# Attention scores: narrow products joined, the forget bias moved to the key side, and a different split of buffers

## The chip, the cores and the metric

The kernel runs on one core of one Trainium2 chip. Its time is device microseconds of one launch; three runs are given by their median. A profile of one more execution of the same program is the source of every row below. The engines are TensorE (PE; its weight loads are PEld), VectorE (DVE), ScalarE (ACT), GpSimd (POOL) and SyncE (SP, which here only issues DMAs).

## The reference

Two layers of a hybrid decoder block over 256 tokens, 1024 features. Each layer: a half-step SwiGLU FFN, a mixing block, a second half-step FFN, a gated per-layer input; a final RMSNorm. The mixing block runs an RG-LRU branch beside a forgetting attention of 8 heads of 128:

```python
log_f = jax.nn.log_sigmoid((f_logit + f_b).astype(jnp.float32))
dcum = jnp.cumsum(log_f, axis=1).transpose(0, 2, 1)
s = jnp.einsum('bhqd,bhkd->bhqk', qb, kh).astype(jnp.float32) * scale
s = s + dqb[..., None] - dcum[:, :, None, :]
s = jnp.where(kpos[None, :] <= qpos[:, None], s, -jnp.inf)
pr = jax.nn.softmax(s, axis=-1).astype(vh.dtype)
return jnp.einsum('bhqk,bhkd->bhqd', pr, vh)
```

The bias of a score is the difference of two cumulative sums, one of the query's position and one of the key's. A softmax over the keys does not change when a number that depends on the query alone is added to its row.

## The kernel before

**Precision.** Every f32 operand is split into a high part (rounded to the matmul's input type) and the low rest: ACT writes the high part, DVE subtracts it to get the low one. A product is then three matmuls, high by high, high by low, low by high. Where high and low of the moving operand lie side by side in one 512-column tile, two matmuls do (`mm2`, lines 344 to 347: one of 512 columns, one of 256), else three of 256 (`mm3`, lines 304 to 306).

**Weights.** `Weights` streams all weight matrices through SBUF in the order of a plan of 238 chunks, 1024 KB each, or 704 KB for the FFNs' output matrices. SP loads a chunk into a raw buffer (tag `wr`, line 84, three buffers); ACT and DVE split it in two units (lines 95 and 96) into one of five pairs of unit buffers (`wh`, `wl`); PE reads the pairs, 4 units behind the splits. A raw buffer is free for the next load when DVE has ended its second split; a unit buffer when PE has read it. Two more matrices per layer (`apart`, line 101, tile `wra`) pass through the same raw buffers in the middle of the FFNs' output stages and are split into tiles of their own (`wbh`, `wbl`). The first layer's input and first weights (tiles `hd`, lines 184 and 186) use the raw buffers too.

**Attention.** For each head four steps stand between other products (the `filler` products of the gates, tiles `f`, and the last query and key projections, tiles `qk`): `step_a` transposes q and k (tile `tr`) and splits them (tiles `aq`), and makes on ACT (line 702) the weights of the bias product from the cumulative sums; `step_b` makes the scores: for the first 128 queries four matmuls against 128 keys, for the second 128 queries four against 256 keys, each time three of `mm3` and one with the bias (line 711). Only keys that a block can see are computed, so the first block has half the columns. DVE then masks and takes the row minimum in one operation (line 715), ACT takes the exponential and its sum (line 717), DVE multiplies by the reciprocal of the sum (line 721, twice). `step_c` transposes the probabilities (tile `pt`, line 729), `step_d` multiplies by v.

**Order.** The order of each engine's instructions is not the order of the code: a scheduler plays the program through with its own model of times and buffers and writes each engine's queue. Each queue then runs strictly in that order, and an instruction that waits holds up all that stand behind it on its engine.

Of the kernel before, what the change touches and what calls it, by code (L numbers as in the profile page):

```python
# [10 lines left out]
F32 = mybir.dt.float32  # L11
F32R = mybir.dt.float32r
AF = mybir.ActivationFunctionType
ALU = mybir.AluOpType
AX = mybir.AxisListType

P = 128
# [102 lines left out]
def trunk(ctx: ExitStack, tc: tile.TileContext, head, xT, pT, vec, w1i, w1o, wf, wqk, wv, wg, wro, wao, wo, w2i, w2o,  # L120
# [12 lines left out]
    def nm(s):  # L133
        cnt[0] += 1
        return f"{s}{cnt[0]}"
# [2 lines left out]
        return bp.tile(shape, dt, name=nm(s), tag="big")  # L138

    def work(dt=F32, s="w"):  # L140
        return kp.tile([P, 256], dt, name=nm(s), tag="w", bufs=12)

    def work2(dt=F32, s="w2"):
        return kp.tile([P, 512], dt, name=nm(s), tag="w2", bufs=3)

    def small(n, s="s", tag="small"):
        return kp.tile([P, n], F32, name=nm(s), tag=tag, bufs=16)
# [12 lines left out]
    for l in range(DEPTH):  # L160
# [8 lines left out]
        plan += [(w2i[l, j], [1024, 1024]) for j in range(FT)]  # L169
        plan += [(w2o[l, m, :, h * 1408:(h + 1) * 1408], [768, 640]) for m in range(KT) for h in range(2)]  # L170
        plan += [(wpg[l, c], [1024, 1024]) for c in range(4)]
    W = Weights(nc, wp, plan, ahead=4, raw_bufs=3, unit_bufs=5, big=big)


    x = cp.tile([P, KT, S], F32, name="x")
# [1 line left out]

    hd = []
    for i in range(KT // 2):
        t = wp.tile([P, 2, HC], F32, name=f"hd{i}", tag="wr", bufs=W.raw_bufs)  # L180
        hd += [t[:, 0], t[:, 1]]
        if i == 0:
            for k in range(2):
                nc.sync.dma_start(out=t[:, k], in_=head[:, k])
        else:
            nc.sync.dma_start(out=t, in_=head[:, 2 * i:2 * i + 2])
# [13 lines left out]

    tri = cp.tile([P, S], F32R, name="tri")

    acol = cp.tile([P, NH], F32, name="acol")
    mcol = cp.tile([P, NH], F32, name="mcol")
    grp = cp.tile([P, 4], F32, name="grp")
    sel = cp.tile([P, 3], F32, name="sel")
    lfh = cp.tile([P, TT, P], F32R, name="lfh")
    lfl = cp.tile([P, TT, P], F32R, name="lfl")
    NRX = 3
# [24 lines left out]
    def constants():  # L234
        G.memset(mask, 0.0)
        G.affine_select(out=mask[:, P:], in_=mask[:, P:], pattern=[[-1, P]], compare_op=ALU.is_ge, fill=BIG,
                        base=0, channel_multiplier=1)
        trif = work(s="trif")
        G.memset(trif, 1.0)
        G.affine_select(out=trif[:, :P], in_=trif[:, :P], pattern=[[1, P]], compare_op=ALU.is_ge, fill=0.0,  # L240
                        base=0, channel_multiplier=-1)
        G.memset(lfh.bitcast(F32), 0.0)
        G.memset(lfl.bitcast(F32), 0.0)
        for t in rxp:
            G.memset(t[:, 0:3], 0.0)
        V.tensor_copy(out=tri, in_=trif)
        yield
        V.tensor_tensor(out=acol, in0=ident[:, 0:NH], in1=ident[:, 32:32 + NH], op=ALU.add)
        V.tensor_tensor(out=mcol, in0=ident[:, 64:64 + NH], in1=ident[:, 96:96 + NH], op=ALU.add)
        V.tensor_scalar(out=mcol, in0=mcol, scalar1=-1.0, scalar2=None, op0=ALU.mult)  # L250
        yield
        for g in range(4):
            V.tensor_reduce(out=grp[:, g:g + 1], in_=ident[:, 32 * g:32 * g + 32], axis=AX.X, op=ALU.add)
        yield
        V.tensor_tensor(out=sel[:, 0:1], in0=grp[:, 1:2], in1=grp[:, 3:4], op=ALU.add)
        V.tensor_scalar(out=sel[:, 0:1], in0=sel[:, 0:1], scalar1=-1.0, scalar2=None, op0=ALU.mult)
        V.tensor_tensor(out=sel[:, 1:2], in0=grp[:, 0:1], in1=grp[:, 1:2], op=ALU.add)
        V.tensor_tensor(out=sel[:, 2:3], in0=grp[:, 2:3], in1=grp[:, 3:4], op=ALU.add)
        yield
        V.tensor_scalar(out=half, in0=vt[:, :, HALF0:], scalar1=0.5, scalar2=None, op0=ALU.mult)  # L260
        for l in range(DEPTH):
            V.tensor_tensor(out=gqk[:, l:l + 1], in0=vt[:, l, VEC["gq"]:VEC["gq"] + 1],
                            in1=vt[:, l, VEC["gk"]:VEC["gk"] + 1], op=ALU.mult)
            ls = small(KT)
            yield from log_sigmoid(ls, vt[:, l, VEC["lam"]:VEC["lam"] + KT], KT)
            yield
            V.tensor_scalar(out=sp[:, l, 0], in0=ls, scalar1=-4.0, scalar2=None, op0=ALU.mult)
            V.tensor_scalar(out=sp[:, l, 1], in0=ls, scalar1=4.0, scalar2=None, op0=ALU.mult)
# [234 lines left out]
    def mix(l, n, wgp):  # L503
# [101 lines left out]
            tick(2)  # L605


        dc = kp.tile([P, S], F32R, name=nm("dc"), tag="dc", bufs=1)
        dk = kp.tile([P, S], F32R, name=nm("dk"), tag="dk", bufs=1)

        def forget():
            lf = kp.tile([P, TT * NH], F32, name=nm("lf"), tag="lf", bufs=1)
            yield from log_sigmoid(lf, z, TT * NH)
            yield
            lf3 = lf.rearrange("p (t o h) -> p t o h", t=TT, o=1)
            for t in range(TT):
                oh = lfh[:, t].rearrange("p (g c) -> p g c", g=4)[:, :, 0:NH]
                ol = lfl[:, t].rearrange("p (g c) -> p g c", g=4)[:, :, 0:NH]
                V.tensor_copy(out=oh, in_=lf3[:, t].to_broadcast([P, 4, NH]))
                V.tensor_tensor(out=ol, in0=lf3[:, t].to_broadcast([P, 4, NH]), in1=oh.bitcast(F32), op=ALU.subtract)  # L620
            yield
            yield
            dps = atbank("dc")
            T.matmul(dps[:, 0:S], lhsT=lfh[:, 0], rhs=tri, start=True, stop=False, skip_group_check=True)
            T.matmul(dps[:, 0:S], lhsT=lfl[:, 0], rhs=tri, start=False, stop=False, skip_group_check=True)
            T.matmul(dps[:, P:S], lhsT=lfh[:, 1], rhs=tri[:, 0:P], start=False, stop=False, skip_group_check=True)
            T.matmul(dps[:, P:S], lhsT=lfl[:, 1], rhs=tri[:, 0:P], start=False, stop=True, skip_group_check=True)
            dh = work(F32R, "dh")
            A.activation(out=dh, in_=dps[:, 0:S], func=AF.Copy)
            V.scalar_tensor_tensor(out=dc, in0=dh.bitcast(F32), scalar=sel[:, 0:1], in1=dps[:, 0:S], op0=ALU.mult,  # L630
                                   op1=ALU.add)
            V.tensor_scalar(out=dk, in0=dc.bitcast(F32), scalar1=sel[:, 1:2], scalar2=sel[:, 2:3], op0=ALU.mult,
                            op1=ALU.add)


        qk = [None, None]
# [50 lines left out]
        def step_a(h):  # L687
            s = st[h]
            cb, hh = h // 4, h % 4
            ps = atbank("tr")  # L690
            for w in range(2):
                for t in range(TT):
                    T.transpose(ps[:, (w * TT + t) * P:(w * TT + t + 1) * P], qk[cb][:, w, t, hh * P:(hh + 1) * P], ident)
            s["q"] = qh, ql = awork(S, "aq", 5), awork(S, "aq", 5)
            s["k"] = kh, kl = awork(S, "aq", 5), awork(S, "aq", 5)
            s["b"] = awork(S, "aq", 5)
            g = gqk[:, l:l + 1]
            A.activation(out=qh, in_=ps[:, 0:S], func=AF.Copy)
            A.activation(out=kh, in_=ps[:, S:], func=AF.Copy, scale=g)
            V.tensor_tensor(out=ql, in0=ps[:, 0:S], in1=qh.bitcast(F32), op=ALU.subtract)  # L700
            V.scalar_tensor_tensor(out=kl, in0=ps[:, S:], scalar=g, in1=kh.bitcast(F32), op0=ALU.mult, op1=ALU.subtract)
            A.activation(out=s["b"], in_=dc.bitcast(F32), func=AF.Identity, scale=mcol[:, h:h + 1], bias=acol[:, h:h + 1])

        def step_b(h):
            s = st[h]
            (qh, ql), (kh, kl), bl = s["q"], s["k"], s["b"]
            ps = atbank("s")
            for t, o, nk in ((0, 0, P), (1, P, S)):
                q = slice(t * P, (t + 1) * P)
                mm3(ps[:, o:o + nk], qh[:, q], ql[:, q], kh[:, 0:nk], kl[:, 0:nk], True, False)  # L710
                T.matmul(ps[:, o:o + nk], lhsT=bl[:, q], rhs=dk[:, 0:nk], start=False, stop=True)
            sv = pr = awork(384, "pr", 2, F32)
            mx, rs = small(TT, "mx", "sa"), small(TT, "rs", "sa")
            for t, o, nk in ((0, 0, P), (1, P, S)):
                V.tensor_tensor_reduce(out=sv[:, o:o + nk], in0=ps[:, o:o + nk], in1=mask[:, S - nk:S], scale=1.0,
                                       scalar=3e38, op0=ALU.add, op1=ALU.min, accum_out=mx[:, t:t + 1])
                A.activation(out=pr[:, o:o + nk], in_=sv[:, o:o + nk], func=AF.Exp, scale=-1.0, bias=mx[:, t:t + 1],
                             accum_out=rs[:, t:t + 1])
            V.reciprocal(out=rs, in_=rs)
            for t, o, nk in ((0, 0, P), (1, P, S)):  # L720
                V.tensor_scalar(out=pr[:, o:o + nk], in0=pr[:, o:o + nk], scalar1=rs[:, t:t + 1], scalar2=None,
                                op0=ALU.mult)
            s["p"] = pr

        def step_c(h):
# [309 lines left out]
```

## Time and profile before

| | |
|---|---|
| median of three runs | 1322.99 us (1322.96 to 1323.09) |
| the profiled execution | 1323.63 us |
| its span, first to last instruction | 1321.8 us |
| PE busy, DVE busy, ACT busy | 99%, 81%, 62% |
| mean granted TensorE clock | 0.997 |
| DMA | 240.21 MB, mean 182 GB/s |

The profiled execution is 0.64 us over the median, and 1.8 us of it lie around the span. A busy share of PE is a weak sign by itself, since matmuls overlap in the pipeline and the end of each is modelled; the distance from one start to the next is what a matmul costs the stream.

### The profile page before, as it was taken

How to read it: one execution, taken by the hardware profiler on the slowest of the kernel's cores; microseconds unless marked ns; L12 is line 12 of the kernel's file. 1: busy time of each engine (PE TensorE's matmuls, PEld its weight loads, DVE VectorE, ACT ScalarE, POOL GpSimd, SP SyncE). 2: the span in 40 equal slices, each digit the busy share in tenths (PEclk: the TensorE clock that was granted, in tenths of full speed). 3: DMA queues.
4: the chain of work that ended last, by engine and by line, in shares of the span. 5: the costliest groups of instructions: out<-in, count | busy, mean ns of one | idle time of the engine just before them, and what ended most of it. 6: DMA issues, size and time to landing. Idle time of an engine off the chain costs nothing.

```text
span 1321.8 us, 22442 instructions
## 1 busy us (share of the span) xinstructions
PE 1311.8 (99%) x8610; PEld 1197.7 (91%) x8610; DVE 1076.1 (81%) x2142; ACT 815.5 (62%) x1470; POOL 34.1 (3%) x43
## 2 busy tenths in 40 slices
PE   9999999999999999999999999999999999999997
PEld 8888899889999888889988888998999998888897
DVE  7998769899757899876789877698997678988756
ACT  6665656868655666565566555578677556655653
POOL 1000000020000000000000000000200000000000
PEclk9999999999999999999999999999999999999998
DMA  8654665445435555456545546644543455554650
GB/s 292 243 179 160 212 225 193 158 164 175 151 128 191 196 189 189 162 184 231 187 165 192 188 153 212 241 161 159 193 166 128 161 190 191 192 191 142 213 187 33
DMA packets 37259, 240.21 MB, mean 182 GB/s; under 512 B 4128, under 2 KB 4768, under 8 KB 14368
## 3 DMA queue, kind: packets, MB, share of 16 engines
q1 hardware_dynamic: 36720, 238.25, 51.3%
q8 instruction: 68, 1.11, 0.3%
q10 hardware_dynamic: 432, 0.52, 0.1%
q14 instruction: 39, 0.32, 0.1%
HBM read 237.71 MB, written 1.05 MB: 181 GB/s over the span
## 4 chain that ended last, share of the span: by engine, by line
PE 99%; DMA 0%; DVE 0%; ACT 0%; SPq 0%; POOLq 0%; issue 0%; DVEq 0%
PE mm L347 20%; PE mm L345 11%; PE at L347 11%; PE at L345 6%; PE f L304 3%; PE f L305 3%; PE f L306 3%; PE qk L309 2%; PE qk L311 2%; PE qk L310 2%; PE mm L306 2%; PE mm L304 2%; PE mm L305 2%; PE ya L347 2%; PE mm L344 2%; PE at L344 2%
## 5 line engine op out<-in xcount | busy, mean ns | idle before, releaser
L95 ACT ACTIVATE wh<-wr 128x1024 fp32r<-128x1024 f32 (+2 forms) x476 | 467.4, 986 | 308.0 <-PE mm L347 90.8
L96 DVE TENSOR_TENSOR wl<-wr,wh 128x1024 fp32r<-128x1024 f32 (+2 forms) x476 | 537.7, 1132 | 142.3 <-ACT wh L95 136.9
L347 PE MATMUL mm<-h,wh 128*128 128x512 f32 x616 | 219.2, 394 | 0.0
L347 PE MATMUL at<-h,wh 128*128 128x512 f32 x616 | 218.4, 394 | 0.0
L345 PE MATMUL mm<-h,wl 128*128 128x256 f32 x704 | 182.4, 281 | 0.0
L345 PE MATMUL at<-h,wl 128*128 128x256 f32 x704 | 181.7, 281 | 0.3 <-DVE wl L96 0.2
L347 PE MATMUL mm<-f,wh 128*128 128x512 f32 x504 | 176.8, 394 | 0.0
L345 PE MATMUL mm<-f,wl 128*128 128x256 f32 x528 | 144.0, 280 | 0.0
L345 PEld LDWEIGHTS at<-h,wl 128*128 128x128 f32 x704 | 131.8, 188 | 8.8 <-DVE wl L96 0.8
L345 PEld LDWEIGHTS mm<-h,wl 128*128 128x128 f32 x704 | 131.8, 188 | 7.8 <-DVE wl L96 0.4
L347 PEld LDWEIGHTS mm<-h,wh 128*128 128x128 f32 x616 | 115.6, 188 | 22.5
L347 PEld LDWEIGHTS at<-h,wh 128*128 128x128 f32 x616 | 114.9, 188 | 21.9
L347 PEld LDWEIGHTS mm<-f,wh 128*128 128x128 f32 x504 | 94.4, 188 | 20.8
L304 PE MATMUL f<-h,wh 128*128 128x256 f32 x384 | 108.6, 283 | 0.0
L306 PE MATMUL f<-h,wl 128*128 128x256 f32 x384 | 108.4, 282 | 0.0
L305 PE MATMUL f<-h,wh 128*128 128x256 f32 x384 | 108.4, 282 | 0.0
L345 PEld LDWEIGHTS mm<-f,wl 128*128 128x128 f32 x528 | 99.4, 188 | 2.1
L305 PEld LDWEIGHTS f<-h,wh 128*128 128x128 f32 x384 | 72.3, 188 | 0.1
L304 PEld LDWEIGHTS f<-h,wh 128*128 128x128 f32 x384 | 72.3, 188 | 0.1
L306 PEld LDWEIGHTS f<-h,wl 128*128 128x128 f32 x384 | 72.4, 189 | 0.0
L381 ACT ACTIVATE sum<-mm 128x256 f32<-128x256 f32 x112 | 40.2, 376 | 49.3 <-PE mm L347 49.3
L382 DVE TENSOR_TENSOR sum<-mm,sum 128x256 f32<-128x256 f32 x112 | 44.9, 417 | 15.0 <-ACT sum L381 15.0
(291 smaller groups left out, 2857.6 us busy)
## 6 DMA issues: line engine op xcount, KB each, us to landing
wr<-in_w2i SPq DMA_DIRECT2D x44, 1024.0 KB, 4.8
wr<-in_w1i SPq DMA_DIRECT2D x41, 1024.0 KB, 4.8
wr<-in_wf SPq DMA_DIRECT2D x32, 1024.0 KB, 4.8
wr<-in_w1o SPq DMA_DIRECT2D x32, 704.0 KB, 4.0
wr<-in_w2o SPq DMA_DIRECT2D x32, 704.0 KB, 4.0
wr<-in_wqk SPq DMA_DIRECT2D x16, 1024.0 KB, 4.8
wr<-in_wv SPq DMA_DIRECT2D x8, 1032.0 KB, 4.9
wr<-in_wro SPq DMA_DIRECT2D x8, 1024.0 KB, 4.8
```

The source lines that it names most:

```text
L95: self.nc.scalar.activation(out=hi[:, c], in_=src[:, c], func=AF.Copy)
L96: self.nc.vector.tensor_tensor(out=lo[:, c], in0=src[:, c], in1=hi[:, c].bitcast(F32), op=ALU.subtract)
L304: T.matmul(ps, lhsT=wh, rhs=xh, start=first, stop=False)
L305: T.matmul(ps, lhsT=wh, rhs=xl, start=False, stop=False)
L306: T.matmul(ps, lhsT=wl, rhs=xh, start=False, stop=last)
L309: T.matmul(ps, lhsT=xh, rhs=wh, start=first, stop=False)
L310: T.matmul(ps, lhsT=xh, rhs=wl, start=False, stop=False)
L344: T.matmul(ps, lhsT=wh, rhs=t, start=True, stop=False, skip_group_check=True)
L345: T.matmul(ps[:, 0:S], lhsT=wl, rhs=t[:, 0:S], start=False, stop=False, skip_group_check=True)
L347: T.matmul(ps, lhsT=wh, rhs=t, start=False, stop=last, skip_group_check=True)
L381: A.activation(out=o, in_=ps[:, S:], func=AF.Copy)
L382: V.tensor_tensor(out=o, in0=ps[:, 0:S], in1=o, op=ALU.add)
```

## The change

Five edits.

1. *Scores.* The two query blocks of a head share one PSUM bank: columns 0 to 255 for the second block, 256 to 383 for the first block's high-by-high sum, 384 to 511 for its high-by-low sum. Six matmuls take the place of eight: four of 256 columns (one of them with the moving operand in two runs of 128, k high and k low beside each other in the new tile `ak`), one of 128, and one of 384 for the bias of both blocks. DVE adds the sum of columns 384 to 511 to the mask first (new tile `m0`) and masks with that.
2. *Bias.* Only the key's part is added. The weights of that product are a column of a constant (`pick`) read 128 times over, the same for all queries; the per-head ACT operation of line 702 is gone, and `dk` has 384 columns.
3. *Probabilities* are scaled by ACT instead of DVE.
4. *Raw weight buffers*: two instead of three; the `hd` tiles move to the pool `big`.
5. *Work tiles*: 16 instead of 12 of 256 columns, 5 instead of 3 of 512. The q split has two buffers of its own, the k split one tile.

```diff
     def work(dt=F32, s="w"):
-        return kp.tile([P, 256], dt, name=nm(s), tag="w", bufs=12)
+        return kp.tile([P, 256], dt, name=nm(s), tag="w", bufs=16)
...
     def work2(dt=F32, s="w2"):
-        return kp.tile([P, 512], dt, name=nm(s), tag="w2", bufs=3)
+        return kp.tile([P, 512], dt, name=nm(s), tag="w2", bufs=5)
...
-    W = Weights(nc, wp, plan, ahead=4, raw_bufs=3, unit_bufs=5, big=big)
+    W = Weights(nc, wp, plan, ahead=4, raw_bufs=2, unit_bufs=5, big=big)
...
-        t = wp.tile([P, 2, HC], F32, name=f"hd{i}", tag="wr", bufs=W.raw_bufs)
+        t = big([P, 2, HC], F32, f"hd{i}")
...
+        V.tensor_tensor(out=pick, in0=ident[:, 0:NH], in1=ident[:, 32:32 + NH], op=ALU.add)
+        V.tensor_reduce(out=neglo, in_=ident[:, 32:64], axis=AX.X, op=ALU.add)
+        V.tensor_scalar(out=neglo, in0=neglo, scalar1=-1.0, scalar2=None, op0=ALU.mult)
...
-            V.scalar_tensor_tensor(out=dc, in0=dh.bitcast(F32), scalar=sel[:, 0:1], in1=dps[:, 0:S], op0=ALU.mult,
-                                   op1=ALU.add)
-            V.tensor_scalar(out=dk, in0=dc.bitcast(F32), scalar1=sel[:, 1:2], scalar2=sel[:, 2:3], op0=ALU.mult,
-                            op1=ALU.add)
+            for o, n_ in ((0, S), (S, P)):
+                V.scalar_tensor_tensor(out=dk[:, o:o + n_], in0=dh[:, 0:n_].bitcast(F32), scalar=neglo,
+                                       in1=dps[:, 0:n_], op0=ALU.mult, op1=ALU.add)
...
-            A.activation(out=s["b"], in_=dc.bitcast(F32), func=AF.Identity, scale=mcol[:, h:h + 1], bias=acol[:, h:h + 1])
...
-            for t, o, nk in ((0, 0, P), (1, P, S)):
-                q = slice(t * P, (t + 1) * P)
-                mm3(ps[:, o:o + nk], qh[:, q], ql[:, q], kh[:, 0:nk], kl[:, 0:nk], True, False)
-                T.matmul(ps[:, o:o + nk], lhsT=bl[:, q], rhs=dk[:, 0:nk], start=False, stop=True)
+            def mm(o, w, r, start=False, stop=False):
+                T.matmul(ps[:, o], lhsT=w, rhs=r, start=start, stop=stop, skip_group_check=True)
+            mm(slice(0, S), qh[:, q1], kk[:, 1], start=True)
+            mm(slice(0, S), qh[:, q1], kk[:, 0])
+            mm(slice(0, S), ql[:, q1], kk[:, 0])
+            mm(slice(S, 2 * S), qh[:, q0], kk[:, :, q0])
+            mm(slice(S, S + P), ql[:, q0], kk[:, 0, q0])
+            mm(slice(0, S + P), pick[:, h:h + 1].to_broadcast([P, P]), dk, stop=True)
...
+            V.tensor_tensor(out=m0[:, q0], in0=ps[:, S + P:], in1=mask[:, q1], op=ALU.add)
...
-                V.tensor_scalar(out=pr[:, o:o + nk], in0=pr[:, o:o + nk], scalar1=rs[:, t:t + 1], scalar2=None,
-                                op0=ALU.mult)
+                A.activation(out=pr[:, o:o + nk], in_=pr[:, o:o + nk], func=AF.Copy, scale=rs[:, t:t + 1])
```

Three places of the queues. On PE, the score products of the first head (moving operand first, then the weights; `aq` are q and k parts, `ak` the joined k). The eight matmuls before:

```order
L304 MATMUL s_3314<-aq_3290,aq_3288 128x128
L305 MATMUL s_3314<-aq_3291,aq_3288 128x128
L306 MATMUL s_3314<-aq_3290,aq_3289 128x128
L711 MATMUL s_3314<-dk_2886,aq_3292 128x128
L304 MATMUL s_3314<-aq_3290,aq_3288 128x256
L305 MATMUL s_3314<-aq_3291,aq_3288 128x256
L306 MATMUL s_3314<-aq_3290,aq_3289 128x256
L711 MATMUL s_3314<-dk_2886,aq_3292 128x256
```

and the six now, which stand without a break:

```order
L700 MATMUL s_3300<-ak_3279,aq_3277 128x256 x2
L700 MATMUL s_3300<-ak_3279,aq_3278 128x256
L700 MATMUL s_3300<-ak_3279,aq_3277 128x256
L700 MATMUL s_3300<-ak_3279,aq_3278 128x128
L700 MATMUL s_3300<-dk_2875,pick 128x384
```

Four narrow products have become one, and one of 384 columns has come in.

On ACT, the first head's probabilities (`pr`) between splits of weights (`wh`). Before:

```order
L717 ACTIVATE pr_3323,rs_3325<-pr_3323,mx_3324 128x128
L95 ACTIVATE wh_3544<-wr_3542 128x1024
L717 ACTIVATE pr_3323,rs_3325<-pr_3323,mx_3324 128x256
L764 ACTIVATE sq_3451<-sq_3451 128x256
L762 ACTIVATE sq_3510<-g_3508 128x256
L95 ACTIVATE wh_3611<-wr_3542 128x1024
```

and now:

```order
L714 ACTIVATE pr_3307,rs_3309<-pr_3307,mx_3308 128x128
L95 ACTIVATE wh_3463<-wr_3402 128x1024
L714 ACTIVATE pr_3307,rs_3309<-pr_3307,mx_3308 128x256
L758 ACTIVATE sq_3434<-g_3432 128x256
L95 ACTIVATE wh_3524<-wr_3522 128x1024
L718 ACTIVATE pr_3307<-pr_3307,rs_3309 128x128
L718 ACTIVATE pr_3307<-pr_3307,rs_3309 128x256
L760 ACTIVATE sq_3434<-sq_3434 128x256
```

The two scalings now stand behind the first split of a fresh chunk (`wr_3522`, the same chunk as `wr_3542` before), that is, behind the landing of its load.

On ACT, in the first FFN's output stage, where the matrix that is loaded apart passes. Before:

```order
L95 ACTIVATE wh_1748<-wr_1746 128x768
L95 ACTIVATE wbh_1789<-wra 128x1024 x2
L95 ACTIVATE wh_1764<-wr_1746 128x640
L381 ACTIVATE sum_1778<-mm_1713 128x256
L95 ACTIVATE wh_1798<-wr_1796 128x768
```

and now:

```order
L95 ACTIVATE wh_1738<-wr_1736 128x768
L95 ACTIVATE wh_1754<-wr_1736 128x640
L371 ACTIVATE sum_1768<-mm_1703 128x256
L95 ACTIVATE wbh_1779<-wra 128x1024 x2
L327 ACTIVATE h_1625<-x,vt 128x256
L388 ACTIVATE sq_1774<-x 128x256
L95 ACTIVATE wh_1788<-wr_1786 128x768
```

The splits of `wra` have moved three instructions back, behind the chunk that is loaded before it; the next chunk (`wr_1786`, before `wr_1796`) follows them as it did.

## Rows read from the trace of the kernel before

**Rows 1.** The page: span, the engines (busy us, share of the span, instructions) and the granted TensorE clock in 40 slices of the span, in tenths of full speed.

```profile
span 1321.8 us, 22442 instructions
PE 1311.8 (99%) x8610; PEld 1197.7 (91%) x8610; DVE 1076.1 (81%) x2142; ACT 815.5 (62%) x1470; POOL 34.1 (3%) x43
PEclk9999999999999999999999999999999999999998
```

**Rows 2.** Everything that PE waited for in the whole span: line, releaser, us in total, times, longest.

```profile
PE warm L871 <- POOL ones L189: 1.1, 1, 1.1
PE fin L933 <- DVE xg L931: 0.9, 1, 0.9
PE st L927 <- DVE facc L923: 0.4, 1, 0.4
PE at L345 <- DVE wl L96: 0.2, 1, 0.2
PE at L344 <- ACT wh L95: 0.2, 1, 0.2
```

**Rows 3.** The timeline of PE at seven of the first head's eight score products (start us, us, engine, line, output and inputs, output's shape), and the first product behind them.

```profile
292.74 0.22 PE L305 MATMUL s<-aq,aq 128*128 128x128 f32 x1
292.80 0.28 PE L306 MATMUL s<-aq,aq 128*128 128x128 f32 x1
292.91 0.28 PE L711 MATMUL s<-dk,aq 128*128 128x128 f32 x1
293.02 0.33 PE L304 MATMUL s<-aq,aq 128*128 128x256 f32 x1
293.19 0.28 PE L305 MATMUL s<-aq,aq 128*128 128x256 f32 x1
...
293.43 0.28 PE L711 MATMUL s<-dk,aq 128*128 128x256 f32 x1
293.54 0.28 PE L305 MATMUL f<-h,wh 128*128 128x256 f32 x1
```

**Rows 4.** The timeline of PE where products of 256 and 512 columns alternate (five pairs from the first row to the last).

```profile
430.00 0.28 PE L345 MATMUL o<-mg,wl 128*128 128x256 f32 x1
430.11 0.40 PE L347 MATMUL o<-mg,wh 128*128 128x512 f32 x1
...
431.74 0.29 PE L345 MATMUL o<-mg,wl 128*128 128x256 f32 x1
```

**Rows 5.** Groups of instructions by line and shape on DVE and ACT (busy us, mean ns of one, then idle time before them): the scaling of the probabilities, the weights of the bias product, the exponentials, and an addition that reads PSUM.

```profile
L721 DVE TENSOR_SCALAR pr<-pr,rs 128x256 f32<-128x256 f32 x16 | 5.5, 346 | 0.0
L721 DVE TENSOR_SCALAR pr<-pr,rs 128x128 f32<-128x128 f32 x16 | 4.5, 282 | 0.3
L702 ACT ACTIVATE aq<-dc,acol,mcol 128x256 fp32r<-128x256 f32 x16 | 9.6, 599 | 0.0
L717 ACT ACTIVATE pr<-pr,mx 128x256 f32<-128x256 f32 x16 | 8.0, 498 | 0.0
L717 ACT ACTIVATE pr<-pr,mx 128x128 f32<-128x128 f32 x16 | 6.4, 399 | 6.1 <-DVE mx L715 6.1
L382 DVE TENSOR_TENSOR sum<-mm,sum 128x256 f32<-128x256 f32 x112 | 44.9, 417 | 15.0 <-ACT sum L381 15.0
```

**Rows 6.** Busy time in the stretch in which the attention of the first layer starts (length, PE, PEld, DVE, ACT, POOL, granted clock, DMA share, GB/s).

```profile
264.00:300.00 36.00, 36.00 (x204) 31.11 (x203) 32.97 (x65) 23.72 (x33) 9.24 (x6) 1.00 0.50 178
```

**Rows 7.** DMA issues of two kinds of chunk (count, KB each, median us from issue to landing), and the landing times of the four matrices loaded apart.

```profile
wr<-in_w1i SPq DMA_DIRECT2D x41, 1024.0 KB, 4.8
wr<-in_w1o SPq DMA_DIRECT2D x32, 704.0 KB, 4.0
...
DMA to landing us min/median/max: 4.8/5.1/5.2
```

**Rows 8.** The timeline in the first FFN's output stage, rows of DVE, SP, ACT and PE: a chunk's second split, a load that is issued at its end, the splits of the matrix loaded apart, the splits of a 768-column unit, and the first use by PE of the low part of the second chunk loaded after it.

```profile
148.69 0.83 DVE L96 TENSOR_TENSOR wl<-wr,wh 128x640 fp32r<-128x640 f32 x1
...
149.54 0.33 SPq L84 DMA_DIRECT2D wr<-in_w1o  x1
...
150.80 2.01 ACT L95 ACTIVATE wbh<-wra 128x1024 fp32r<-128x1024 f32 x2 [0.30 <-DMA wra<-in_wg]
151.90 2.36 DVE L96 TENSOR_TENSOR wbl<-wra,wbh 128x1024 fp32r<-128x1024 f32 x2 [0.40 <-ACT wbh L95]
...
161.41 0.84 ACT L95 ACTIVATE wh<-wr 128x768 fp32r<-128x768 f32 x1
162.35 0.95 DVE L96 TENSOR_TENSOR wl<-wr,wh 128x768 fp32r<-128x768 f32 x1
...
164.79 0.28 PE L345 MATMUL mm<-f,wl 128*128 128x256 f32 x1
```

**Rows 9.** The first head's probabilities: the timeline of DVE's scaling and of the first transposition on PE.

```profile
300.59 0.54 DVE L721 TENSOR_SCALAR pr<-pr,rs 128x128 f32<-128x128 f32 x2
...
301.96 0.27 PE L729 MATMUL pt<-ident,pr 128*128 128x128 f32 x1
```

**Rows 10.** The start of the program: the loads of the first tiles (of three issues, the last waits for a free buffer), and a wait of ACT for one of them.

```profile
1.71 6.01 SPq L186 DMA_DIRECT2D hd<-in_head  x3
...
7.42 0.51 ACT L337 ACTIVATE h<-hd 128x256 fp32r<-128x256 f32 x1 [0.51 <-DMA hd<-in_head]
```

More of the change, by code (lines that the diff above doesn't have):

```diff
@@ L201, in trunk @@
     tri = cp.tile([P, S], F32R, name="tri")
[L203 to L206, printed above, removed]
+    neglo = cp.tile([P, 1], F32, name="neglo")
+    pick = cp.tile([P, NH], F32R, name="pick")
     lfh = cp.tile([P, TT, P], F32R, name="lfh")
@@ L247, in constants @@
         yield
[L248 to L258, printed above, removed]
+        V.tensor_tensor(out=pick, in0=ident[:, 0:NH], in1=ident[:, 32:32 + NH], op=ALU.add)
+        V.tensor_reduce(out=neglo, in_=ident[:, 32:64], axis=AX.X, op=ALU.add)
+        V.tensor_scalar(out=neglo, in0=neglo, scalar1=-1.0, scalar2=None, op0=ALU.mult)
         yield
@@ L605, in mix @@
             tick(2)
-        dc = kp.tile([P, S], F32R, name=nm("dc"), tag="dc", bufs=1)
-        dk = kp.tile([P, S], F32R, name=nm("dk"), tag="dk", bufs=1)
+        dk = kp.tile([P, S + P], F32R, name=nm("dk"), tag="dk", bufs=1)
         def forget():
@@ L616, in forget @@
             for t in range(TT):
[L617 to L620, printed above, removed]
+                oh = lfh[:, t].rearrange("p (g c) -> p g c", g=4)[:, 0:2, 0:NH]
+                ol = lfl[:, t].rearrange("p (g c) -> p g c", g=4)[:, 0:2, 0:NH]
+                V.tensor_copy(out=oh, in_=lf3[:, t].to_broadcast([P, 2, NH]))
+                V.tensor_tensor(out=ol, in0=lf3[:, t].to_broadcast([P, 2, NH]), in1=oh.bitcast(F32), op=ALU.subtract)
             yield
@@ L693, in step_a @@
                     T.transpose(ps[:, (w * TT + t) * P:(w * TT + t + 1) * P], qk[cb][:, w, t, hh * P:(hh + 1) * P], ident)
-            s["q"] = qh, ql = awork(S, "aq", 5), awork(S, "aq", 5)
-            s["k"] = kh, kl = awork(S, "aq", 5), awork(S, "aq", 5)
-            s["b"] = awork(S, "aq", 5)
+            s["q"] = qh, ql = awork(S, "aq", 2), awork(S, "aq", 2)
+            s["k"] = kk = kp.tile([P, 2, S], F32R, name=nm("ak"), tag="ak", bufs=1)
+            kh, kl = kk[:, 0], kk[:, 1]
             g = gqk[:, l:l + 1]
@@ L701, in step_a @@
             V.scalar_tensor_tensor(out=kl, in0=ps[:, S:], scalar=g, in1=kh.bitcast(F32), op0=ALU.mult, op1=ALU.subtract)
-            A.activation(out=s["b"], in_=dc.bitcast(F32), func=AF.Identity, scale=mcol[:, h:h + 1], bias=acol[:, h:h + 1])
         def step_b(h):
             s = st[h]
-            (qh, ql), (kh, kl), bl = s["q"], s["k"], s["b"]
+            (qh, ql), kk = s["q"], s["k"]
+            q0, q1 = slice(0, P), slice(P, S)
             ps = atbank("s")
-            for t, o, nk in ((0, 0, P), (1, P, S)):
-                q = slice(t * P, (t + 1) * P)
-                mm3(ps[:, o:o + nk], qh[:, q], ql[:, q], kh[:, 0:nk], kl[:, 0:nk], True, False)
-                T.matmul(ps[:, o:o + nk], lhsT=bl[:, q], rhs=dk[:, 0:nk], start=False, stop=True)
+            def mm(o, w, r, start=False, stop=False):
[6 more added lines that the diff above has]
+            mm(slice(0, S + P), pick[:, h:h + 1].to_broadcast([P, P]), dk, stop=True)
             sv = pr = awork(384, "pr", 2, F32)
             mx, rs = small(TT, "mx", "sa"), small(TT, "rs", "sa")
-            for t, o, nk in ((0, 0, P), (1, P, S)):
-                V.tensor_tensor_reduce(out=sv[:, o:o + nk], in0=ps[:, o:o + nk], in1=mask[:, S - nk:S], scale=1.0,
+            m0 = work(s="m0")
+            V.tensor_tensor(out=m0[:, q0], in0=ps[:, S + P:], in1=mask[:, q1], op=ALU.add)
+            for t, o, nk, pc, mk in ((0, 0, P, slice(S, S + P), m0[:, q0]), (1, P, S, slice(0, S), mask)):
+                V.tensor_tensor_reduce(out=sv[:, o:o + nk], in0=ps[:, pc], in1=mk, scale=1.0,
                                        scalar=3e38, op0=ALU.add, op1=ALU.min, accum_out=mx[:, t:t + 1])
```

## The prediction

> **What bounds the kernel now.** I read the page first, then the waits of PE, then its timeline inside the attention, then the queues of DVE, ACT and SP at the places where the change makes them tighter. The page has PE busy over the whole span, at a granted clock that is full in all but the last slice [rows 1], and the reader should not trust a busy share alone. The waits settle it: in the whole span PE waited for others five times, 1.1 + 0.9 + 0.4 + 0.2 + 0.2 = 2.8 us, all of them in the first microseconds or the last ones [rows 2]. Between them PE never waits, so the time is the sum of what each matmul costs PE's stream, plus a start and an end that the change leaves alone. From this follows what can help: only work taken from PE. DVE and ACT can cost something if they get late, but can give nothing back.
>
> What a matmul costs is the distance from its start to the next one's. In rows of 256 and 512 columns, five pairs take 431.74 - 430.00 = 1.74 us, 0.348 a pair [rows 4]; Two score products of 256 columns in a row take 293.43 - 293.19 = 0.24 us [rows 3], from rows of two decimals; I use 0.118 for one, so 512 columns take 0.348 - 0.118 = 0.230. For 128 columns single distances mislead (0.06 before one, 0.17 after it), because the record starts while the weights are still coming. I take the whole piece: from 292.74 to 293.54 stand three products of 128 and four of 256 columns, 0.80 us; less 4 x 0.118 this leaves 0.109 each [rows 3]. So half the columns save almost nothing: a narrow product costs 0.11, hardly less than one twice as wide.
>
> **The change part by part.**
>
> *Scores.* Before, a head pays 4 x 0.110 + 4 x 0.118 = 0.912 us. After, four of 256, one of 128 and one of 384: the columns are the same 1536, but the number of products falls from eight to six. The trace has no product of 384 columns; the rows on either side of it are 0.118 and 0.230, and since the cost between them grows with the columns I take the middle, 0.174, and say 0.175. Sum: 4 x 0.118 + 0.110 + 0.175 = 0.757. The head saves 0.155 us, the 16 heads 2.5 us. The ends: with 0.118 for the wide one 3.4 us, with 0.230 1.6 us. Two forms are new. The moving operand in two runs of 128 costs 0.118 if runs do not matter and at most what two products of 128 cost, 0.22, which would take back 16 x 0.10 = 1.6 us; the weights that are one column read 128 times cost nothing extra if a load is a load, and at most a second load time, 0.11, which takes back 1.8 us. Nothing in the rows shows either as different from a plain tile, so I take none of it.
>
> The trace has a narrow product at 0.109 and a wide one at 0.230 [rows 3, 4]. The Trainium skill, page "TensorE: Matmul & The Clock Gate", section "Back-to-back issue gap", gives for a sustained stream about 81 ns at 128 columns and 131 ns at 512; by it a head would save about 3 x 81 - 114 = 129 ns (114 being an estimate between its two figures) and the 16 heads 2.1 us. The rows of this case lie far above both figures, so I go by the rows.
>
> *Bias.* ACT loses 16 operations of 599 ns [rows 5], PE keeps the product, DVE has two operations on the cumulative sums as before. ACT is not what PE waits for: worth nothing.
>
> *Probabilities.* DVE loses 16 x (346 + 282) ns = 10.0 us, ACT gains 16 x (about 498 + 399) = 14.4 us by its exponentials of the same shapes, and DVE gains the sum with the mask, between 282 ns (128 columns from SBUF) and 417 (256 from PSUM), 4.5 to 6.7 us [rows 5]. All of it lies beside PE's stream. The cover is thin where the attention starts: there DVE is busy 32.97 of 36 us [rows 6]. For the first head DVE ends its scaling at 300.59 + 0.54 = 301.13 and PE transposes at 301.96 [rows 9], 0.8 us to spare. After the change the scaling stands on ACT behind the split of a chunk, whose load now starts one chunk later. The scheduler has shifted PE's work with it, so I cost it at nothing, and at most at 0.9 us (the two scalings) in each layer.
>
> *Two raw buffers.* A load now starts when the chunk two before it, not three, has been split. Take the FFN's output stage, where chunks are small. PE needs 22 pairs x 0.348 = 7.66 us for an output tile, which is two chunks. One buffer's loop is load 4.0 [rows 7], some 0.1 until ACT starts, and two splits one after the other, 0.84 + 0.95 + 0.83 = 2.6 us [rows 8]: 6.7 us for every two chunks. It fits, with 0.9 us to spare. With the large chunks it is 4.8 + 0.1 + 3.5 (the splits of a large one [rows 8]) against 16 pairs a chunk, 11.1 us for two.
>
> The place with least to spare is where the matrix loaded apart passes, four times in the program. Its load would start at 149.54, when the chunk two before has been split (148.69 + 0.83), and land 5.1 us later at 154.64 [rows 7, 8]. Its splits end 151.90 + 2.36 - 150.80 = 3.46 us after ACT starts them, so at 158.2; then the second chunk behind it can load, lands at 162.2, and is split by 162.3 + 0.84 + 0.95 = 164.1. PE wants it at 164.79 [rows 8]. That leaves 0.7 us. If both loads take 5.2, the longest of rows 7, it is 165.4, a stall of 0.6 us, four times 2.4. I take none, and keep it for the range.
>
> The loads' price decides here; rows 7 have 4.0 us for 704 KB. The Trainium skill, page "DMA: Bandwidth & Descriptors", fits a load as a fixed 2.0 us and its bytes at 436 GB/s; that is 3.7 us for 704 KB, an estimate by which there would be 0.3 us more to spare at each such place. The rows are dearer than the fit, and I use the rows.
>
> *The start.* The third large load of `hd` waits in SP for a buffer now [rows 10] and will not any more, and the first weight chunks are issued at once behind it. But the first waits of PE there sum to 0.4 us [rows 2], and ACT's wait at 7.42 is for a load that nothing held up [rows 10]: 0 to 0.4 us of gain, taken as nothing. *More work tiles* loosen what PE does not wait for: nothing.
>
> The sum is -2.5 us. The profiled execution, 1323.6 (span 1321.8 and 1.8 around it), would become 1321.1; it lay 0.6 over the median of the runs, so the median goes from 1323.0 to 1320.5 us. That is 0.19%, and 0.2%, 2.65 us, is about what a measurement of this kernel can tell from no change: the forecast lies just inside that line, at 1320.3.
>
> **The rivals.**
>
> *The joining saves more, 1319.9 us.* If the wide product costs 0.165 instead of 0.175 the heads save 2.7 us, and if the start gives its 0.4 the sum is 3.1. For it: a wide product hides the next weight load entirely. Against: the 512-column rows show the full price per column.
>
> *Local stalls eat it, 1322.2 us.* The four places of the matrix loaded apart and the two first heads give back some 1.7 us of the 4.2 that they could at most. For it: spare times of 0.7 and 0.8 us by rows. Against: the queues were laid out with two buffers in mind.
>
> *The new weights do not load like others, 1322.3 us.* A second load time per head is 1.8 us. This is the case in which the change does not do what it says.
>
> *Slower: the output stages run out of weights, 1328 us.* One mechanism: a load that takes longer, because loads now start later and fall together, makes a buffer's loop longer than PE's 7.66 us. It decides at a landing time of 7.66 - 2.7 = 4.96 us. At 5.2 each of 32 output tiles loses 0.24 us, 7.7 in all, and the sum is 1320.5 + 7.7. For it: rows 7 have landings of 5.2, for larger loads. Against: the median is 4.0, and with two buffers fewer loads are in flight, not more.
>
> **How the numbers follow.** The forecast 0.45, more saved 0.38, local stalls 0.06, dear weights 0.04, starved stages 0.07. Only the second is faster by over 0.2%, only the last slower by it: 0.38, 0.55, 0.07. The likeliest is 1320.5. The range goes down a little beyond the second case, towards the low price of the wide product (1319.6), to 1319.5, and up over the local stalls and the dear weights, to 1322.5.
>
> **What would show it.** The score products of a head should take about 0.76 us on PE from the first start to the next product's, the one of 384 columns 0.17 to 0.18. PE's waits should still stand at the two ends alone; any wait on `wl`, `wh` or `pr` between them is a local stall, and where it stands says which. The loads of SP should show shorter times from landing to first split. I am wrong if the 384-column product or the strided one has a price of its own, or if PE waits inside the FFNs' output stages.

## The result, and the profile after

The changed kernel takes 1336.65 us (median of 5 runs, 1335.92 to 1337.90), the one before 1323.03 (5 runs). The ratio is 1.0102 with a 95% interval of 1.0091 to 1.0113: slower by 13.6 us, where a gain of 2.5 us had been forecast and the range ended at 1322.5. The profiled execution took 1336.66 us. Of the runs below, e6 and e10 each had one execution of over 1830 us, which their ratios leave out.

The page of after, the rows that answer to [rows 1]:

```profile
span 1334.9 us, 22346 instructions
PE 1312.5 (98%) x8578; PEld 1194.7 (89%) x8578; DVE 1074.2 (80%) x2118; ACT 816.8 (61%) x1486; POOL 34.1 (3%) x43
PEclk9999999999999999999999999999999999999999
```

The clock is as full as it was and no engine has noticeably more work (ACT 1.3 us, PE 0.7, DVE less); the span has grown by 13.1 us. The waits of PE in the whole span, line and releaser, total, times and longest, are the rows to set beside [rows 2]:

```profile
PE f L294 <- DVE g L755: 7.5, 6, 1.7
PE s L700 <- ACT yr L324: 1.4, 2, 0.7
PE o L735 <- ACT ph L727: 1.2, 2, 0.6
PE at L335 <- DVE wl L96: 1.1, 2, 0.8
...
PE pt L725 <- ACT pr L718: 0.4, 1, 0.4
```

Before, PE waited only in the first and the last microseconds of the span. Now it waits in the middle, most of all in front of `f`, the filler products that stand between the heads, for `g`, the operation of DVE that empties a filler's PSUM bank. The windows of the changed kernel say where (stretch, its length, then busy time of PE, PEld, DVE, ACT and POOL, the clock, DMA); the last row is the second stretch before the change:

```profile
300.00:340.00 40.00, 37.92 (x316) 36.98 (x315) 36.70 (x91) 31.72 (x78) 0.00 (x0) 1.00 0.45 157
340.00:400.00 60.00, 56.90 (x433) 54.08 (x432) 39.70 (x78) 36.20 (x74) 0.00 (x0) 1.00 0.40 141
...
340.00:400.00 60.00, 60.00 (x464) 57.72 (x463) 39.91 (x84) 36.86 (x75) 0.00 (x0) 1.00 0.37 131
```

PE stands idle for 2.1 + 3.1 = 5.2 us of these 100, and nowhere in the FFNs' output stages. What is telling is that DVE is not full there: in the second stretch it is idle for a third of the time, as it was before, while PE waits for it. An engine with time to spare that is late points to the order of its work. One such wait, all engines, in order of time:

```profile
335.73 0.28 PE L296 MATMUL f<-h,wl 128*128 128x256 f32 x1
...
346.00 1.06 ACT L95 ACTIVATE wh<-wr 128x1024 fp32r<-128x1024 f32 x1 [1.32 <-PE f L295]
...
346.55 0.75 PE L700 MATMUL s<-ak,aq 128*128 128x256 f32 x5
...
347.09 1.23 DVE L96 TENSOR_TENSOR wl<-wr,wh 128x1024 fp32r<-128x1024 f32 x1 [1.17 <-ACT wh L95]
347.14 0.40 PE L700 MATMUL s<-dk,pick 128*128 128x384 f32 x1
...
348.23 0.42 DVE L325 TENSOR_TENSOR ot<-o,ot 128x256 fp32r<-128x256 f32 x1
...
348.56 0.28 DVE L710 TENSOR_TENSOR m<-s,mask 128x128 f32<-128x128 f32 x1
348.76 0.75 DVE L755 TENSOR_TENSOR g<-f,RB 128x256 f32<-128x256 f32 x2
...
349.23 0.39 PE L294 MATMUL f<-h,wh 128*128 128x256 f32 x1 [1.26 <-DVE g L755]
```

The first row is the last product of the twelfth filler, through at 335.73 + 0.28. Its bank could be emptied from then on, and there are four such banks, so the sixteenth filler needs it (the last row). But its `g` comes at 348.76, 12.7 us later, together with the next one and directly behind `m`, the new sum of a head's scores with the mask (`m0` in the code, line 709). `m` can only run when the score products are through (347.14 + 0.40), and ahead of it DVE has waited 1.17 us for a split on ACT. DVE works off its list in order. The Trainium skill, "PSUM — Partial Sum Buffer", section "Engine vs sequencer instructions", says of the queues of ScalarE, VectorE and GpSimdE that they are strictly first in, first out; these rows agree, with an operand that lay ready for 12.7 us. And the circle closes through PE: the scores that `m` waits for stand on PE behind the fifteenth filler.

So the question is why `g` stands there. I counted in the order of DVE's instructions, first layer, where the 24 evictions `g` (0 to 23) and the 8 sums (M) stand:

```
changed:            M 0 M 1 2 M 3 4 5 M 6 7 M 8 9 10 M 11 12 M 13 14 15 M 16 17 18 ...
m0 in own tiles:    M 0 1 2 3 4 M 5 6 7 M 8 9 10 11 12 M 13 14 15 M 16 17 18 M 19 20 M 21 22 23 M
```

Each number is one eviction. The first line is exactly the order in which the program's text asks for these tiles: `m0` and `g` both come from the 16 rotating work tiles (`work()`, one tag), and as soon as they share it none passes the other, although nothing but the tag connects them. The number of tiles is not what makes this order: it is the same in e2 and e4 below, where 12 tiles rotate and not 16. The second line is the same kernel with `m0` in tiles of its own: from the second head on the sums come four to eight evictions later, when their scores are there. In the kernel before, every `g` stands behind the weight split of the fourth unit after its own; in the changed one behind that of the third to the eighth.

### The profile page after: what moved, and what is told of

The parts are those of the page before. It is cut to its first block, busy times and chain, and to the rows that moved or that the text cites. A ratio compares the mean times of both kernels' runs of the same rounds, so it can differ in the third digit from the quotient of the medians.

```text
span 1334.9 us, 22346 instructions
## 1 busy us (share of the span) xinstructions
PE 1312.5 (98%) x8578; PEld 1194.7 (89%) x8578; DVE 1074.2 (80%) x2118; ACT 816.8 (61%) x1486; POOL 34.1 (3%) x43
## 4 chain that ended last, share of the span: by engine, by line
PE 94%; DVE 3%; DMA 1%; ACT 1%; issue 0%; SPq 0%; POOLq 0%; DVEq 0%; ACTq 0%
PE mm L337 19%; PE mm L335 11%; PE at L337 11%; PE at L335 6%; PE f L294 3%; PE f L295 3%; PE f L296 3%; PE qk L299 2%; PE qk L301 2%; PE qk L300 2%; PE mm L295 2%; PE mm L296 2%; PE mm L294 2%; PE ya L337 2%; PE mm L334 2%; PE at L334 1%
```

## The experiments

Theories: **the tie** (the shared work tiles hold `g` behind `m0`), against **rival one** (two raw buffers make the splits late) and **rival two** (ACT has too much with the scaling). The "before" of each difference is the kernel before on the same chip, 1323.0 to 1323.7 us.

**e1, m0 in its own tiles.**

```diff
-            m0 = work(s="m0")
+            m0 = awork(P, "m0", 2, F32)
```

> The changed kernel, but the sum m0 gets tiles of its own (two of 128 columns) in place of one from the 16 rotating work tiles. Tie theory: the sum is handed its work tile ahead of the next filler's g, so g cannot be placed before it on DVE, and in the changed program every g stands behind m0, which waits for the score products; without the shared tiles g goes back to its place, PE's waits on g vanish, and the time is what the joining promised: 1320.5 us (1319.5 to 1322.5), some 16 us under the changed kernel. Rival one (two raw buffers: ACT's splits wait for loads and DVE's queue is late with them): nothing of that is touched, 1335 to 1338. Rival two (ACT is overloaded with the scaling of the probabilities): 1334 to 1338.

Measured 1325.61, ratio 1.0015 (1.0006 to 1.0024). Each against the kernel before on its own chip, this one line takes away 11.3 of the 13.6 us, and PE has no wait for `g` left. The tie is the cause of most, and neither rival is, since both had left the time at 1334 us or more. But the time stays above the range that I gave, 2.3 us over before and not 2.5 under. Beside the first weights of the program (2.3 us, see under *The start*), PE's waits show two places, twice each (once in a layer):

```profile
PE ya L334 <- ACT wh L95: 1.6, 2, 0.8
PE pt L725 <- ACT pr L718: 1.4, 2, 0.7
```

**e2, three raw buffers in the changed kernel.**

```diff
-tag="w", bufs=16)
+tag="w", bufs=12)
-tag="w2", bufs=5)
+tag="w2", bufs=3)
-raw_bufs=2
+raw_bufs=3
```

> The changed kernel with three raw weight buffers again (and 12 and 3 work tiles, so that they fit); m0 stays on the work tiles. Tie theory: g still stands behind m0, the time stays within 1333 to 1339 us. Rival one (two raw buffers): the 13.6 us go, 1320 to 1323. Rival two (ACT overloaded): 1333 to 1338.

Measured 1339.91, 1.0123 (1.0109 to 1.0137), 0.9 us over the range of the tie, with 11.4 us of waits for `g`:

```profile
PE f L294 <- DVE g L755: 11.4, 8, 1.7
```

Neither the two buffers nor the greater number of work tiles are what costs; the waits even grew. Rival one falls.

**e3, two raw buffers in the kernel before** (`raw_bufs=2`, and line 180 of after, which takes the head's loads out of them).

> The kernel before with two raw weight buffers and the head's loads moved out of them, nothing else. Tie theory and the prediction: 1322.5 to 1324.5, the loads stay hidden. Rival one: 1330 to 1338, with PE waits in the filler stretch.

Measured 1323.66, 1.0002 (0.9993 to 1.0010). What the page of waits shows for it is a lesson by itself. Two kinds of chunk, ACT's waits for their loads:

```profile
ACT wh L95 <- DMA wr<-in_wf: 23.3, 14, 4.3
ACT wh L95 <- DMA wr<-in_w1o: 23.2, 19, 3.1
```

ACT waits over 100 us in all for loads, which in the kernel before had nearly always lain ready (the largest such row there is 3.2 us). The time does not change beyond its interval, and PE still waits only at the two ends; the split weights that PE has in stock cover it.

**e4, the kernel before with a copy in a shared work tile; e5, with the same copy in a tile of its own** (`awork(P, "m0", 1, F32)` in the first line).

```diff
+            m0 = work(s="m0")
+            V.tensor_copy(out=m0[:, 0:P], in_=ps[:, 0:P])
-            for t, o, nk in ((0, 0, P), (1, P, S)):
-                V.tensor_tensor_reduce(out=sv[:, o:o + nk], in0=ps[:, o:o + nk], in1=mask[:, S - nk:S], scale=1.0,
+            for t, o, nk, sc in ((0, 0, P, m0[:, 0:P]), (1, P, S, ps[:, P:384])):
+                V.tensor_tensor_reduce(out=sv[:, o:o + nk], in0=sc, in1=mask[:, S - nk:S], scale=1.0,
```

> The kernel before, with its eight narrow products, three raw buffers and the scaling on DVE; added is one copy of the first 128 columns of a head's scores into a rotating work tile, from which the row maximum of that half is then taken. Tie theory: this alone puts g behind the copy, PE waits on g in the filler stretch as in the changed kernel: 1333 to 1341 us (1323 plus some 16). Rivals one and two: one more DVE operation of about 0.28 us a head beside PE, 1323 to 1325.

> The kernel before with the same added copy of 128 score columns as in the run that put it into a shared work tile (1343.3 us), but into a tile of its own. Tie theory: only the sharing costs, so 1322.8 to 1324.3, no PE wait in the filler stretch. Rival (the DVE operation itself makes g late): 1335 to 1343.

e4 takes 1343.27, 1.0148 (1.0134 to 1.0162): 20 us more, 2 over the upper end expected, for 16 copies of 281 ns (e5's row) beside PE. e5, the same instructions with another tag, takes 1326.07, 1.0021 (1.0012 to 1.0030). PE's waits for `g` in e4, and the one wait in e5 that lies inside the attention:

```profile
PE f L304 <- DVE g L761: 14.0, 8, 1.9
...
PE pt L731 <- DVE pr L723: 0.9, 2, 0.5
```

So the tie alone slows the kernel before, without any other part of the change. Not all of the 20 us are waiting, though. Once in each layer, behind its third (352.1) and its fourth wait (1034.8), the granted clock of e4 falls from 1.00 to 0.50, the lower of its two levels (1.2 GHz), for 3.4 us. These are its windows at the first fall and behind it, and the one such stretch in e6 below:

```profile
352.10:355.50 3.40, 3.40 (x18) 3.40 (x17) 1.13 (x6) 0.75 (x3) 0.00 (x0) 0.50 0.60 248
355.50:359.00 3.50, 3.50 (x32) 3.50 (x31) 1.53 (x2) 1.55 (x2) 0.00 (x0) 1.00 0.00 0
...
389.80:393.20 3.40, 3.40 (x12) 2.88 (x11) 0.11 (x1) 0.00 (x0) 0.00 (x0) 0.50 0.00 0
```

In the first one fifteen products of 256 columns take 355.35 - 352.15 = 3.20 us from start to start, 0.21 each and not 0.12. By that I estimate a loss of 1.5 us a stretch, 3 us of e4's 20. No other profile of this case shows such a stretch before its last microseconds.

But e5 missed too: the copy itself costs 2.6 us, and PE waits before the last head's transposes. That is the same end of the attention where e1 waits at `ya`.

**e6, e1 with three raw buffers** (the edit of e2 on top of e1)**; e7, e1 with the scaling on DVE** (the loop at line 718 as before)**; e8, the joining alone** (both, and the head's loads in the raw buffers).

> The changed kernel with m0 in its own tiles and three raw buffers (12 and 3 work tiles); the scaling stays on ACT, the head's loads outside the raw buffers. With m0 in its own tiles alone it was 1325.6, with PE waits before the transposes of the first head (0.7 each layer) and at ya (0.8 each layer). If both come from the two raw buffers (ACT's split waits for a load and the scaling stands behind it) they go: 1325.6 - 3.0 = 1322.6, or 1321.5 to 1323. If the scaling on ACT alone makes them, they stay: 1325 to 1326.

> The changed kernel with m0 in its own tiles and the probabilities scaled on DVE again; two raw buffers stay. If the first head's transposes wait because the scaling stands behind a split on ACT, that 0.7 a layer goes (1.4 us): 1323.5 to 1324.8. If the wait only moves to DVE, 1325 to 1326.

> The joined score products and the key's bias alone: scaling on DVE, three raw buffers, head's loads in them, 12 and 3 work tiles, m0 in its own tiles. By the sum of the prediction (16 heads, 0.155 each) 1323.2 - 2.5 = 1320.7, PE waiting at the two ends alone. If interleaving with the transposes or the strided product takes it back: 1322 to 1323.5.

All three missed, each by being too fast in the forecast: 1328.15, 1.0031 (1.0020 to 1.0043); 1327.92, 1.0033 (1.0021 to 1.0045); 1329.82, 1.0045 (1.0033 to 1.0057). What I had expected of the first head did come true: its wait before `pt` is gone in all three, whichever of the two parts was undone. But the waits at `ya`, the first output projection, grew (e1 1.6, e6 2.4, e7 and e8 3.3 us); in e6 the stretch at the lower clock comes on top. The joining alone, the one part that was to bring the gain, is 6.4 us slower than before:

```profile
PE o L334 <- DVE sum L372: 2.6, 2, 1.3
PE ya L334 <- ACT wh L95: 1.8, 2, 0.9
PE ya L335 <- DVE wl L96: 1.5, 2, 0.8
```

The timeline of e8 there, ACT, DVE and PE:

```profile
383.49 0.39 PE L337 MATMUL ya<-yr,wh 128*128 128x512 f32 x1
383.91 1.06 ACT L95 ACTIVATE wh<-wr 128x1024 fp32r<-128x1024 f32 x1 [1.85 <-PE ya L337]
384.23 0.75 PE L700 MATMUL s<-ak,aq 128*128 128x256 f32 x5
...
385.01 1.23 DVE L96 TENSOR_TENSOR wl<-wr,wh 128x1024 fp32r<-128x1024 f32 x1 [1.69 <-ACT wh L95]
...
386.29 0.50 PE L335 MATMUL ya<-yr,wl 128*128 128x256 f32 x2 [0.77 <-DVE wl L96]
...
390.93 0.40 PE L334 MATMUL yb<-ot,wh 128*128 128x512 f32 x1
```

A unit's weights are split (383.91) only when PE has finished the `ya` unit before it, and PE wants them at once: of the five tiles for split weights only one still turns. The next in the program's order are the units of `yb`, which need the output of all eight heads, and the last head has just got its scores at 384.23; in the kernel before that was at 376.52. PE takes `ya` units past them, and the split `yb` units sit on their tiles until `yb` begins at 390.93. That they hold the tiles is read from this order, not from a row of its own. The new theory, **the late head**: the sum with the mask (288 ns, plus its place in DVE's queue) stands in each head's chain, eight heads add it up, and the last one comes too late. It asks for an edit that touches no work at all, only when heads start.

**e9, e10, e11: e8, e1 and e6 with the heads every 2.25 filler units** in place of every 2.5:

```diff
-            slots[4 + (5 * h + 1) // 2 + i].append((f, h))
+            slots[4 + (9 * h) // 4 + i].append((f, h))
```

> The joined products alone (1329.8 us) with the heads started every 2.25 filler units in place of every 2.5, so that the last head is done sooner; in the order of PE its second output group comes after 764 filler and output products of the stretch instead of 803 (before the change: 781). Late-head theory: the chain of a head is longer by the sum with the mask, the last head comes late, the output products that need it hold their weight tiles, and PE waits at ya (1.8 and 1.5 us) and o (2.6 us); with the last head early these go and the joining gives what was forecast: 1320 to 1322. Rival (the joined products cost PE more when transposes stand among them, or DVE is simply too slow): 1327 to 1331.

> The changed kernel with m0 in its own tiles (1325.6 us) and the heads every 2.25 units: two raw buffers, scaling on ACT, more work tiles as in the change. Late-head theory: the waits at ya (1.6 us) go, the one before the first head's transposes (1.4 us) stays, 1323 to 1324.5. Rival: 1325 to 1327.

> As the run before, with three raw buffers and 12 and 3 work tiles (without the spacing 1328.2 us, PE waiting 2.4 us at ya alone). Late-head theory: 1320 to 1322, PE waiting at the two ends alone; then the two raw buffers are what makes the first head's transposes wait. Rival: 1326 to 1329.

e9 1321.32, 0.9984 (0.9975 to 0.9993); e10 1322.18, 0.9988 (0.9979 to 0.9997); e11 1321.01, 0.9981 (0.9972 to 0.9990). The joining alone fell by 8.7 us (each against its own kernel before) and now beats the kernel before by 2.3; e11, the whole change but for the two raw buffers and the extra work tiles, by 2.6. The waits at `ya` and `o` are gone. All that PE waits for in e9:

```profile
PE warm L868 <- POOL ones L189: 1.1, 1, 1.1
PE fin L930 <- DVE xg L928: 0.9, 1, 0.9
PE st L924 <- DVE facc L920: 0.4, 1, 0.4
PE at L335 <- DVE wl L96: 0.3, 1, 0.3
```

and the last head's scores in e9, 12.7 us sooner than in e8:

```profile
371.58 0.69 PE L700 MATMUL s<-ak,aq 128*128 128x256 f32 x5
```

e10, with two raw buffers, came out 0.8 us under the range expected; of the wait at the first head 0.9 us is left, in one layer only and at another product (`o`, for `ph` and `pl`).

**e12, the kernel before with the scaling on ACT alone.**

> The kernel before with the probabilities scaled on ACT, nothing else. The prediction costed this at nothing: 1322.7 to 1323.9. If ACT's longer chain makes the last head late, PE waits at ya: 1325 to 1327.

Measured 1323.66, 1.0002 (0.9993 to 1.0010): nothing, as forecast.

**e13, the changed kernel with the new spacing alone; e14, the kernel before with it** (the edit of e9)**; e15, the joined products without the sum**: e8 with

```diff
-            mm(slice(S, 2 * S), qh[:, q0], kk[:, :, q0])
+            mm(slice(S, S + P), qh[:, q0], kk[:, 1, q0])
+            mm(slice(S, S + P), qh[:, q0], kk[:, 0, q0])
-            m0 = awork(P, "m0", 2, F32)
-            V.tensor_tensor(out=m0[:, q0], in0=ps[:, S + P:], in1=mask[:, q1], op=ALU.add)
```

and the row maximum taken from PSUM and the mask again.

> The changed kernel with nothing but the spacing of the heads (every 2.25 units); m0 stays on the shared work tiles. Tie theory: g still stands behind m0, PE still waits on g: 1331 to 1337. If the late last head were the whole cause: 1321 to 1324.

> The kernel before with nothing but the spacing. PE does not wait in it, so there is nothing to gain: 1322.8 to 1324.2. If the gain of the joined kernels (1321.0 to 1321.3) came from the spacing and not from the joining: 1320.5 to 1321.8.

> The joined products alone with the old spacing, but the strided product replaced by two of 128 columns, so that the sum m0 falls away (seven products a head, 0.859 by the prices of the prediction, 0.053 less than before, 0.85 us in all). The last head's second output group then stands after 778 products, as before the change (781). Late-head theory: the waits at ya and o of the joined products alone (1329.8) go with the sum: 1322 to 1323.5. If the joining itself makes the heads late: 1326 to 1330.

e13 takes 1328.06, 1.0037 (1.0024 to 1.0049), between the two ranges: the tie still costs, but less than I expected (1331 at least). Its waits for `g` have fallen from 7.5 to 3.5 us:

```profile
PE f L294 <- DVE g L755: 3.5, 5, 1.0
```

A likely reason, not tried by itself, is that the spacing shifts when the sum before a held `g` comes. e13 and e10 are one more pair that differs by the tag alone: 5.1 us over the kernel before against 1.5 under it, so the tie costs 6.5 us with the new spacing. e14 takes 1323.34, 1.0000 (0.9991 to 1.0009): the spacing by itself gives nothing, so the gain of e9 to e11 is the joining's. e15 takes 1322.99, 0.9999 (0.9990 to 1.0008). All that PE waits for in it:

```profile
PE warm L867 <- POOL ones L189: 1.1, 1, 1.1
PE fin L929 <- DVE xg L927: 0.9, 1, 0.9
PE at L335 <- DVE wl L96: 0.5, 1, 0.5
PE st L923 <- DVE facc L919: 0.4, 1, 0.4
```

Without the sum in the chain no wait stands at `ya` or `o` at the old spacing, so it is the sum and not the joining that makes the heads late. The 0.85 us that seven products should have saved lie within that interval and were not seen.

In the kernels with the old spacing the number of filler and projection products that PE's order places ahead of the last head's second output group goes with it: 781 before, 778 in e15, 769 in e12, 748 in e3, all without a wait there; 785 in e5 and e6, 787 in e1, 803 in e7 and e8, all with one at the end of the attention. The changed kernel itself has no wait at `ya`, and its last head gets its scores at 367.05: in the first of the two orders above the sums stand behind fewer evictions than in the second, so the heads run ahead of the fillers. The late head shows only once the tie is gone.

## Why the prediction was wrong, step by step

- **What bounds the kernel: right.** PE's stream was the whole time. The listed waits alone do not add up to it: in the changed kernel they sum to 14.9 us, 12.1 more than before, and with the joining's 2.5 us back that is 9.6, where the span grew by 13.1. A stall costs the stream some 0.16 us more than its idle time, because a product that shows 0.28 us is else followed after 0.12; over 13 new waits that is 2 us. The rest is not broken down.
- **The scores: right.** The first head's six score products in e9, and the transposes behind them:

```profile
292.72 0.70 PE L700 MATMUL s<-ak,aq 128*128 128x256 f32 x5
293.26 0.39 PE L700 MATMUL s<-dk,pick 128*128 128x384 f32 x1
293.49 0.60 PE L681 MATMUL tr<-ident,qk 128*128 128x128 f32 x4
```

From start to start that is 0.77 us, where 0.757 was forecast; the answer to [rows 3]. The one of 384 columns shows 0.23 and the five ahead of it 0.54; with four at 0.118 the narrow one is left 0.07, so that the two together take 0.30 where 0.110 + 0.175 was forecast, and there is no room for a price of the strided one. The gain, 2.5 us by the sum, measured 2.3 (e9) and 2.6 (e11) once nothing stood in its way. The 2.1 us estimated by the Trainium skill ("TensorE: Matmul & The Clock Gate", "Back-to-back issue gap") lies in the intervals of e9 and e11 too; the times cannot choose between the two gains, though the rows of the products lie far above the prices that the 2.1 is made of.
- **The probabilities: the step that failed.** I counted the sum with the mask as "4.5 to 6.7 us" of DVE's time "beside PE's stream" and gave it no price. It measured 288 ns, 16 x 288 = 4.6 us, so the size was right. What was wrong was to price an instruction by its duration. It brought a tile request into a shared rotation, and with it an order (11.3 us with the change's other parts, e1; 17.3 us between e4 and e5, some 3 of them by the clock), and it lengthened every head's chain (2.6 us by e5, 6.4 between e8 and e15). Without the tie and with the heads closer together the whole change gains 1.5 us (e10). Neither cost shows in DVE's busy time, which fell from 1076.1 to 1074.2 us. The first stood in the order of DVE's instructions, where the evictions wait behind the sums; the prediction weighed PE's and ACT's order, and of DVE only how busy it is.
- **The scaling on ACT: right alone, wrong in company.** e12 costs nothing. With two raw buffers the first head's transposes wait 0.7 us in each layer (e1), within the 0.9 that I had as an upper bound and took as nothing; it takes both parts, since undoing either removes the wait (e6, e7). The rows in e1 show the mechanism as forecast, the scaling behind the split of a chunk that has just landed:

```profile
300.40 1.06 ACT L95 ACTIVATE wh<-wr 128x1024 fp32r<-128x1024 f32 x1 [1.40 <-DMA wr<-in_wf]
301.37 0.78 ACT L718 ACTIVATE pr<-pr,rs 128x128 f32<-128x128 f32 x2
301.81 0.33 PE L725 MATMUL pt<-ident,pr 128*128 128x128 f32 x1 [0.72 <-ACT pr L718]
```

- **Two raw buffers: right.** Alone they cost 0.3 us, with an interval from -0.9 to 1.3 (e3). PE does not wait in the output stages or where a matrix is loaded apart; the loads land in 4.8 and 4.0 us as before [rows 7].
- **The start: not settled.** PE's waits for its first weights sum to between nothing (e13) and 2.3 us (e1) in the profiled executions, and they are as large with the head's loads in the raw buffers (1.9 in e5).
- **The rivals.** "Slower" was there as one mechanism, starved output stages, and that did not happen; the place that fails is the one where engines hand PSUM banks to each other, and I had none for it. "Local stalls" named the first heads rightly: priced at 1.7 us together with the matrices loaded apart, they show 1.4 us of waits in e1.

That the tag is what ties is shown (the changed kernel against e1, e4 against e5, e13 against e10). Why tiles of one tag keep their order, as a rule of the scheduler, is read from the two orders above and was not tried further.

## What to carry to other kernels

A new temporary is not free because its engine has time: ask which rotating tiles it takes and whose request stands behind it, and give a tile that waits for something far away a tag of its own. When the profile shows an engine that is idle and yet late, read the order of its queue before its busy time. And where a chain is repeated, follow its last link to whoever waits for it at the end: here 0.3 us more a head decided over 6 us, and starting the heads a little closer gave back all of it.

## What was not expected of the hardware

ACT can wait for loads for over 100 us (e3) without PE noticing, with five pairs of buffers for split units. In the other direction, evictions held behind an operation of 0.28 us on DVE kept PE waiting for up to 1.9 us at a time (e4). And a stall can cost twice: behind waits of 1.9, 1.6 and 1.6 us in the first layer the granted clock of e4 fell to half for 3.4 us.
